# Triangular inverses of several token groups taken in one call, with other costs in the planner that orders the work, in a gated-DeltaNet and differential-attention step

## Chip, cores and metric

The kernel runs on one core of a Trainium2 chip. The metric is the time on the device in microseconds (us) for one execution of the whole program; the median of several runs counts. TensorE is called PE below, VectorE DVE, ScalarE ACT, GpSimd POOL, and SyncE, which issues most DMAs, SP.

## What is computed

One inference step through two layers, for a prompt of 2048 tokens and 8 samples of 16 tokens, model width 1024, 8 heads of width 128, all in float32. Layer 0 mixes tokens with a gated DeltaNet, layer 1 with differential attention over the prompt and a cache of 512 tokens. Around each mixer stand a modulated RMS norm, input projections, a gate and an output projection. The part the change is about is the delta rule:

```python
def gdn_chunked(q, k, v, g, beta, s0, chunk):
    G = jnp.cumsum(g, axis=-1)
    ...
    A = jnp.where(strict, jnp.einsum("bnhid,bnhjd->bnhij", kb, k) * decay, 0.0)
    eye = jnp.eye(chunk, dtype=q.dtype)
    rhs = jnp.concatenate([v * beta[..., None], kb * jnp.exp(G)[..., None]], axis=-1)
    sol = lax.linalg.triangular_solve(eye + A, rhs, left_side=True, lower=True, unit_diagonal=True)
    u_intra, w = sol[..., :dv], sol[..., dv:]
    ...
    def step(s, xs):
        u_i, w_i, qk_i, qg_i, kd_i, gl_i = xs
        u = u_i - jnp.einsum("bhcd,bhde->bhce", w_i, s)
        o = jnp.einsum("bhcd,bhde->bhce", qg_i, s) + jnp.einsum("bhij,bhje->bhie", qk_i, u)
        s = s * gl_i[..., None, None] + jnp.einsum("bhcd,bhce->bhde", kd_i, u)
        return s, o
    s_final, o = lax.scan(step, s0, xs)
```

For each head and each chunk of tokens a unit triangular matrix has to be inverted (or solved with), and then a state `s` goes through the chunks one after the other.

## The kernel before

**Tiling.** Tokens are cut into tiles of 128 (17 of them, one holds the samples). They are taken in two halves of 9 and 8 tiles. Each half of a layer is cut into groups of up to three tiles: 3, 3, 3 in the first half, and 3, 3, 2 in the second. The program goes through: start, DeltaNet heads of half 0, output projection, attention heads of half 0, output, DeltaNet heads of half 1, output projection, attention heads of half 1, output. In the trace the DeltaNet heads lie at 85 to 840 us and at 1790 to 2412 us of the span.

**The planner.** Nothing is issued in the order of the source. The class `Weave` holds the work as streams (Python generators) that yield the engine that they need next. `run` (line 281) always takes the stream that could start first (ties by priority), and `account` (line 130) charges each instruction a cost and notes when its result would be ready. The order so found is kept on each engine. Tiles and PSUM banks are taken from counted places (`tile`, `hold`, line 242 on) and are given back with `free`, so a stream can also wait for a place. Every instruction is issued through the wrapper `call` (line 105), so all rows of the profile read L105, and work is told apart by its tiles.

**A DeltaNet half** (`gdn_heads`, line 955). `projections` takes head by head and group by group; a projection is a chain of 128x384 (or 128x256) matmuls of weights `wq` or `wz` and tokens `hT`, and these are by far most of PE's work. Each group spawns `conv`, `keys`, `queries` and `values`; `keys` spawns `inverse` (line 1384) with priority 3.

**One inverse call** is for the one to three tiles of one group and one head:

- `product` makes X, the decayed product of keys, one 128x128 tile at a time.
- X goes to DRAM (area `xd`), and its 16x16 diagonal blocks, 8 for each tile, come back as `Lx`, one block to a lane, so 24 or 16 lanes are in use. `blocks` (line 1335) inverts all blocks at once with a run of 17 DVE instructions on the tiles Lx, Lw, Lt and Lr. The lanes go through DRAM (`wd`) to W16 and, masked, to W.
- PE puts the blocks together to 32, 64 and 128 rows in seven bursts of small matmuls, with ACT and DVE copies between them. In the profile they read `V,X` (32x32, all four quarters), `W,Y` (four quarters), `V,X` and `W,Y` (two quarters), transposes `cst_ident,Wf`, then `F,X` and `Wf,F`. `each` issues a burst quarter by quarter, all tiles of a quarter in a row. A float32 matmul counts twice in the profile and once in a listing of the order.
- The result is Wf, one tile of 128x128 for each token tile.

There are 48 calls: 40 of 3 tiles and 8 of 2.

**The scan** (`scans`, `scan`, line 1481 on, priority 5) then takes a head's tiles one after the other. For each tile PE makes `S,k`; DVE makes y; PE makes `y,Wf`; ACT copies r; PE makes `r,kd`; DVE makes the next state S; `S,q` and `r,E` give the output. It starts a group when that group's `inv` event is done (line 1488).

Of the kernel before, what the change touches and what calls it, by code (L numbers as in the profile page):

```python
# [87 lines left out]
class Weave:  # L88
# [23 lines left out]
    def __init__(self, tc, kept):  # L112
# [5 lines left out]
        self.parts = {}  # L118
        self.free_at = dict(pe=0.0, v=0.0, s=0.0, g=0.0, sy=0.0)
# [10 lines left out]
    def account(self, key, op, args, kw):  # L130
# [4 lines left out]
        n = 1  # L135
# [4 lines left out]
        if key == "pe":  # L140
            if op == "transpose":
                c = (2 if rest[0].dtype == F32 else 1) * max(n, out.shape[0]) * 0.417 + 2
            elif rest[0].dtype == F32:
                c = 4 * max(n, rest[0].shape[-1]) * 0.417 / (4 if out.shape[0] <= 32 else 1)
            else:
                c = max(n, 2 * rest[0].shape[-1]) * 0.417 + 2
        elif key == "v":
            fast = op in ("tensor_copy", "tensor_scalar", "memset") and all(a.space != PSUM for a in rest)
            c = 75 + n * (0.52 if fast else 1.04)
            if op in ("scalar_tensor_tensor", "tensor_scalar") and any(a.shape[-1] == 1 for a in rest):  # L150
                c += 60
            if op == "memset":
                c = 60 + 0.26 * n
        elif key == "s":
            c = 60 + 0.83 * n + (95 if "accum_out" in kw else 0)
            if any(isinstance(kw.get(k), bass.AP) for k in ("bias", "scale")):
                c += 85
            elif rest[0].space != PSUM:
                c += 32
        elif key == "g":  # L160
            if op == "memset":
                c = 30 + 0.85 * n
            elif op == "tensor_tensor":
                c = 150 + 2.1 * n
            else:
                c = (240 if len(rest) > 1 else 155) + 0.84 * n
            if op == "tensor_tensor" and kw.get("op") == ALU.pow:
                c = 300 + 160 * n
# [4 lines left out]
        start = self.free_at[key]  # L173
# [157 lines left out]
def body(ctx, tc, I, O):  # L331
# [101 lines left out]
    areas = [[dram.tile([3, n], F32, name=f"{k}{i}") for k, n in (("xd", P * P + P), ("wd", P * 16))] for i in range(2)]  # L433
# [521 lines left out]
    def gdn_heads(hi_, tiles_of, pool, ahead):  # L955
        last = hi_ == len(HALVES) - 1
        NX, NWF, NE, NV, NK, NN, ND, NU = ((3, 3, 4, 2, 5, 3, 4, 3), (3, 3, 5, 2, 6, 6, 5, 4))[hi_]
# [377 lines left out]
        def blocks(area, nl):  # L1335

            X, Wl = (pool.tile([24, 16, 16], F32, name=k, bufs=1) for k in ("Lx", "Lw"))
# [7 lines left out]
            T, R = (pool.tile([24, k], F32, name=nm, bufs=1) for k, nm in ((512, "Lt"), (64, "Lr")))  # L1345
# [38 lines left out]
        def inverse(h, gi, d):  # L1384

            nt = len(tiles_of[gi])
            h0, h1 = slice(0, 64), slice(64, P)
            X = yield from new([P, 3, P], "X", NX, "v")
            yield ("E", h, gi),
            for i in range(nt):  # L1390
# [3 lines left out]
            sy.dma_start(area[0][0:nt, 0:P * P].rearrange("t (p c) -> p t c", c=P), X[:, 0:nt])  # L1394
            yield from blocks(area, 8 * nt)
            W16 = yield from new([P, 3, 16], "W16", 2, "sy")
            sy.dma_start(W16[:, 0:nt], area[1][0:nt].rearrange("t (p c) -> p t c", c=16))
            W.free(area)
            Wt = yield from new([P, 3, 32], "W", 2, "v")
# [5 lines left out]
            V = yield from new([P, 3, 32], "V", 2, "v")  # L1405
            Y = yield from new([P, 3, 32], "Y", 2, "s")
            F = yield from new([P, 3, 64], "F", 2, "s")
# [5 lines left out]
            pa, pb, pf, pt = area_of(0, 32), area_of(96, 32), area_of(192, 64), area_of(0, 64)  # L1413
# [7 lines left out]
            def parts(t, rows, cols=slice(0, 32)):  # L1421
                cols = cols if isinstance(cols, list) else [cols] * len(rows)
                return [t[r, i, c] for r, c in zip(rows, cols) for i in range(nt)]


# [3 lines left out]
            each(parts(pa, quarters), parts(X, quarters, quarters), parts(V, quarters))  # L1429
# [10 lines left out]
            each(parts(pa, lower), parts(X, upper, lower), parts(V, upper))  # L1440
            Wf = d["Wf"] = yield from new([P, 3, P], "Wf", NWF, "g")
            e = W.either(nt * P)
            yield e
            getattr(W, e).tensor_tensor(
                out=Wf[:, 0:nt].rearrange("p t (a c) -> p t a c", c=32),
                in0=Wt[:, 0:nt, None, :].broadcast_to([P, nt, 4, 32]),
                in1=C("quart").rearrange("p (a c) -> p a c", c=32)[:, None].broadcast_to([P, nt, 4, 32]), op=ALU.mult)
# [6 lines left out]
            for r, c in zip(upper, lower):  # L1454
                s.copy(Wf[r, 0:nt, c], pb[r])

            for i in range(nt):
                yield "pe"
                pe.transpose(pf[h0, i], Wf[h0, i, h0], ident[0:64, 0:64])
# [3 lines left out]
            for c in range(64, P, 32):  # L1463
                each(parts(pt, [slice(c, c + 32)], slice(0, 64)), parts(X, [h0], slice(c, c + 32)), parts(F, [h0], h0))
            W.free(X)
            yield "s"
            s.copy(F[h1, 0:nt], pt[h1])
            yield "pe"
            each(parts(pf, [h0], h0), parts(F, [h1], h0), parts(Wf, [h1], h1))
            yield "s"  # L1470
            s.copy(Wf[h0, 0:nt, h1], pf[h0])
            W.free(Wt, V, Y, F, pi)
            W.done(("inv", h, gi))
# [188 lines left out]
    def diff_heads(hi_, tiles_of, pool, ahead):  # L1662
# [133 lines left out]

        def queries(h, gi, d):
            nt = len(tiles_of[gi])
            yield ("conv", h, gi, 0),
            yield ("sq", h, gi),  # L1800
            sq, sm = d["sq"], d["sm"]
            pt = yield from turn(d["q"], nt * P)
            yield from squares(pt, nt * P, sq[:, 1])
            W.free(pt)
            yield "g"
            g.tensor_scalar(sm[:, 3, 0:nt], sq[:, 1, 0:nt], 128.0 * EPS, 512.0 * EPS * EPS, op0=ALU.mult, op1=ALU.add)
            yield ("xq", h, gi),
            W.free(sq)
            for i in range(nt):
                yield from product(d, i, d["q"], d["E"])  # L1810
# [882 lines left out]
```

## Time and profile before

| | |
|---|---|
| median of 3 runs | 3558.8 us (3554.32 to 3575.8) |
| the profiled execution, its own time | 3559.35 us |
| its span, first to last instruction | 3557.6 us |
| mean granted clock of TensorE in it | 0.977 |
| PE busy | 3390.2 us (95%) |
| DVE, ACT, POOL busy | 2531.9 (71%), 1763.0 (50%), 1560.0 us (44%) |

Busy time on PE is time with a matmul in flight. In a view by waits, a row gives the instruction that waited, the one that released it, the time in total, how often, and the longest. In a timeline, a bracket gives the idle time of that engine before the row, and what ended it.

### The profile page before, as it was taken

The numbers are of one execution on the slowest core, as the hardware profiler recorded it, in microseconds if no ns is written. First come the engines' busy times: TensorE is split into PE (matmuls) and PEld (weight loads), VectorE is DVE, ScalarE is ACT, GpSimd is POOL, SyncE is SP. The second block draws the span as 40 slices with busy tenths as digits, with TensorE's granted clock in tenths as the row PEclk, the third lists the DMA queues.
The fourth block names the chain that finished last, engine by engine and source line by source line (L and its number), as shares of the span: only waits on it lengthen the run. The fifth ranks groups of instructions, "written<-read, shape, count | busy, mean of one in ns | idle before, by whom it ended". The sixth has DMA issues, their size and how long they took to land.

```text
span 3557.6 us, 79075 instructions
## 1 busy us (share of the span) xinstructions
PE 3390.2 (95%) x28952; PEld 3151.5 (89%) x28952; DVE 2531.9 (71%) x6462; ACT 1763.0 (50%) x5376; POOL 1560.0 (44%) x2836
## 2 busy tenths in 40 slices
PE   5999999999999999999999999998899999999988
PEld 2887789889999999998989899888898999999988
DVE  4677788776576666666567777775588878888872
ACT  3454455553354444444445555553365555555541
POOL 4344444443444344333434554544444444444432
PEclk6999999999999999999999999998999999999999
DMA  5225432236343333444432222224311112111113
GB/s 191 59 64 169 122 77 69 61 98 195 124 130 112 112 114 114 122 120 136 159 91 50 58 62 74 60 75 161 125 42 49 37 55 57 52 52 41 47 57 125
DMA packets 479420, 330.59 MB, mean 93 GB/s; under 512 B 65799, under 2 KB 442143, under 8 KB 479030
## 3 DMA queue, kind: packets, MB, share of 16 engines
q1 hardware_dynamic: 474358, 316.76, 30.0%
q0 software_dynamic: 4672, 8.78, 1.0%
q8 instruction: 227, 3.72, 0.4%
q14 instruction: 163, 1.34, 0.1%
HBM read 233.65 MB, written 91.77 MB: 91 GB/s over the span
## 4 chain that ended last, share of the span: by engine, by line
PE 37%; DVE 7%; POOL 3%; ACT 2%; issue 2%; DMA 1%; SPq 0%; POOLq 0%; DVEq 0%; ACTq 0%
PE ps L105 37%; DVE p L105 1%; DVE negm L105 1%; DVE Lt L105 1%; POOL sm L105 1%; POOL p L105 1%; POOL fo L105 1%; ACT jkg L105 0%; DVE wq L105 0%; DVE rz L105 0%; DVE Lr L105 0%; DMA st<-in_w_in_diff_dram 0%; ACT L105 0%; DMA ro<-og 0%; ACT at L105 0%
## 5 line engine op out<-in xcount | busy, mean ns | idle before, releaser
L105 PE MATMUL ps<-wq,hT 128*128 128x256 f32 x6120 | 851.4, 287 | 4.2 <-DVE r L105 3.1
L105 PEld LDWEIGHTS ps<-wq,hT 128*128 128x128 f32 x6120 | 775.2, 191 | 16.9 <-DVE r L105 3.5
L105 PE MATMUL ps<-hT,wq 128*128 128x384 f32 (+1 forms) x3456 | 696.4, 341 | 2.7 <-ACT ub L105 2.2
L105 PE MATMUL ps<-wz,hT 128*128 128x256 f32 x4488 | 647.4, 292 | 13.3 <-DVE r L105 12.1
L105 PEld LDWEIGHTS ps<-wz,hT 128*128 128x128 f32 x4488 | 581.9, 194 | 23.6 <-DVE r L105 12.8
L105 PEld LDWEIGHTS ps<-hT,wq 128*128 128x128 f32 x3456 | 557.2, 190 | 15.8 <-ACT ub L105 3.1
L105 ACT ACTIVATE p<-ps,negm 128x512 f32<-128x512 f32 (+3 forms) x640 | 397.1, 624 | 225.5 <-DVE negm L105 220.3
L105 DVE TENSOR_REDUCE negm<-ps 128x1 f32<-128x512 f32 (+3 forms) x640 | 375.0, 606 | 66.6 <-PE ps L105 55.5
L105 PE MATMUL ps<-kst,qst 128*128 128x512 f32 (+3 forms) x1280 | 346.7, 379 | 2.8 <-ACT p L105 2.7
L105 POOL TENSOR_SCALAR p<-p,fj 128x512 f32<-128x512 f32 (+2 forms) x320 | 230.8, 732 | 231.4 <-DVE fj L105 165.5
L105 PE MATMUL ps<-vpc,at 128*128 128x128 f32 x2176 | 294.9, 278 | 7.9 <-ACT at L105 6.2
L105 PEld LDWEIGHTS ps<-vpc,at 128*128 128x128 f32 x2176 | 274.5, 193 | 20.7 <-ACT at L105 10.8
L105 DVE SCALAR_TENSOR_TENSOR p<-p,fj,p 128x512 f32<-128x512 f32 (+2 forms) x320 | 248.4, 803 | 23.3 <-POOL p L105 22.8
L105 ACT COPY at<-ps 128x512 f32<-128x512 f32 (+3 forms) x258 | 132.7, 515 | 234.2 <-PE ps L105 228.9
L105 PEld LDWEIGHTS ps<-kst,qst 128*128 128x128 f32 x1280 | 205.8, 190 | 20.2 <-ACT p L105 6.0
L105 POOL TENSOR_TENSOR wq<-st,wq 128x512 fp32r<-128x512 f32 x110 | 150.5, 1370 | 162.0 <-ACT wq L105 92.0
L105 PE MATMUL ps<-cst_ident,p 128*128 128x128 f32 x1224 | 195.3, 277 | 18.9 <-DVE hT L105 7.9
L105 POOL TENSOR_TENSOR fo<-fo,cpow 128x1 f32<-128x1 f32 x280 | 175.5, 627 | 23.3
L105 ACT ACTIVATE jk<-ps 128x128 f32<-128x128 f32 (+1 forms) x212 | 80.4, 379 | 201.6 <-PE ps L105 145.6
L105 PEld LDWEIGHTS ps<-cst_ident,p 128*128 128x128 f32 x1224 | 144.7, 142 | 27.7 <-DVE hT L105 9.1
L105 POOL TENSOR_SCALAR fo<-so 128x1 f32<-128x1 f32 x144 | 32.3, 224 | 269.0 <-ACT jk L105 255.7
L105 POOL TENSOR_SCALAR fo<-so,sm 128x1 f32<-128x1 f32 x136 | 50.3, 370 | 211.5 <-ACT jkg L105 211.2
(328 smaller groups left out, 6413.2 us busy)
## 6 DMA issues: line engine op xcount, KB each, us to landing
st<-in_w_in_gdn_dram SPq DMA_DIRECT2D x128, 256.0 KB
st<-in_w_in_diff_dram SPq DMA_DIRECT2D x256, 128.0 KB
x<-x SPq DMA_DIRECT2D x34, 512.0 KB
wz<-in_w_ada_dram SPq DMA_DIRECT2D x16, 1024.0 KB
sp<-in_cache_k_dram SPq DMA_DIRECT2D x64, 256.0 KB
sp<-in_cache_v_dram SPq DMA_DIRECT2D x64, 256.0 KB
zg<-zt SPq DMA_DIRECT2D x68, 128.0 KB
og<-o SPq DMA_DIRECT2D x136, 64.0 KB
```

Of the source, the lines that this page charges most:

```text
L105: r = f(*args, **kw)
```

## The change

There are three parts.

1. **Costs in `account`.** PE: a float32r matmul of n columns costs max(n, 192) x 0.434 + 6 ns in place of max(n, twice the weights' columns) x 0.417 + 2; the other PE forms are changed alike, with less for small tiles, and a `hold` of 100 or 120 ns is put ahead of an instruction that changes the tile size of the PE array. DVE: products with a last dimension up to 8 cost twice as much. ACT: 1280 ns for a change of function table. POOL: small operations and powers cost more.
2. **Inverses in batches.** `inverse` now makes X only, and the first group of a batch spawns `invert` for all groups of the batch. Half 0: the first group alone, the second and third together; half 1: all three groups together; head 7 (the last) of either half: each group apart. So there are 27 calls (12 of 3 tiles, 7 of 6, 7 of 8, 1 of 2). Tiles, areas and lanes grow with it (up to 64 lanes), X gets 4 places in place of 3, and the tiles of a call (W16, W, F; V and Y now lie in F) have one place each in place of two. A call's three groups get their Wf together, and are free for the scan together.
3. A second, unused copy of some of the functions is taken out of the source (490 lines; no instruction depends on it).

```diff
@@ account
         if key == "pe":
+            rows, cols = (next(k for k in (32, 64, P) if a <= k) for a in (rest[0].shape[0], rest[0].shape[-1]))
             if op == "transpose":
-                c = (2 if rest[0].dtype == F32 else 1) * max(n, out.shape[0]) * 0.417 + 2
+                c = max(n, out.shape[0]) * (0.85 if rest[0].dtype == F32 else 0.65)
             elif rest[0].dtype == F32:
-                c = 4 * max(n, rest[0].shape[-1]) * 0.417 / (4 if out.shape[0] <= 32 else 1)
+                c = 4 * max(n, rest[0].shape[-1]) * 0.434 / (4 if cols == 32 else 1) / (2 if rows == 32 else 1)
             else:
-                c = max(n, 2 * rest[0].shape[-1]) * 0.417 + 2
+                c = max(n, 192) * 0.434 + 6
+
+            if (rows, cols) != self.tiling:
+                hold = 100 if self.tiling == (P, P) else 120
+                self.tiling = rows, cols
...
+            if op == "tensor_tensor" and len(out.shape) == 4 and out.shape[-1] <= 8:
+                c = 75 + 2.06 * n
...
-        start = self.free_at[key]
+        start = self.free_at[key] + hold
@@ gdn_heads
-        NX, NWF, NE, NV, NK, NN, ND, NU = ((3, 3, 4, 2, 5, 3, 4, 3), (3, 3, 5, 2, 6, 6, 5, 4))[hi_]
+        NX, NWF, NE, NV, NK, NN, ND, NU = ((4, 3, 4, 2, 5, 3, 4, 3), (4, 3, 5, 2, 6, 6, 5, 4))[hi_]
+        NTI = (6, 8)[hi_]
@@ blocks
-            X, Wl = (pool.tile([24, 16, 16], F32, name=k, bufs=1) for k in ("Lx", "Lw"))
+            X, Wl = (pool.tile([8 * NTI, 16, 16], F32, name=k, bufs=1) for k in ("Lx", "Lw"))
@@ inverse
-            X = yield from new([P, 3, P], "X", NX, "v")
+            batch = next(b for b in batches_of(h) if gi in b)
+            if gi == batch[0]:
+                W.spawn(invert(h, batch), 3)
+            X = d["X"] = yield from new([P, 3, P], "X", NX, "v")
...
+        def batches_of(h):
+
+            if h == H - 1:
+                return [[gi] for gi in range(NGr)]
+            return [[0], list(range(1, NGr))] if hi_ == 0 else [list(range(NGr))]
+
+        def invert(h, batch):
+
+            h0, h1 = slice(0, 64), slice(64, P)
+            at = [(gi, i) for gi in batch for i in range(len(tiles_of[gi]))]
+            nt = len(at)
...
+            for gi in batch:
+                yield ("X", h, gi), "sy"
+                n = len(tiles_of[gi])
+                sy.dma_start(area[0][first[gi]:first[gi] + n, 0:P * P].rearrange("t (p c) -> p t c", c=P),
+                             U[h, gi]["X"][:, 0:n])
             yield from blocks(area, 8 * nt)
...
+            F = yield from new([P, NTI, 64], "F", 1, "v")
+            V, Y = (F[:, a * NTI // 2:(a + 1) * NTI // 2].rearrange("p t (a c) -> p (t a) c", c=32) for a in range(2))
...
-            each(parts(pa, quarters), parts(X, quarters, quarters), parts(V, quarters))
+            each(parts(pa, quarters), parts_of("X", quarters, quarters), parts(V, quarters))
...
-            W.done(("inv", h, gi))
+            W.free(Wt, F, pi)
+            for gi in batch:
+                W.done(("inv", h, gi))
```

**What moves, in three places.** PE in half 1, before: the first bursts of a call of three tiles, `V,X` (12 matmuls, and later 6) and `W,Y`, among projections `wz,hT` and `hT,wq`.

```order
L105 MATMUL ps_78<-V_26499,X_25991 32x32 x12
L105 MATMUL ps_81<-wz_26269,hT_22658 128x256 x3
L105 MATMUL ps_79<-S,q_24899 128x128
L105 MATMUL ps_79<-r,E_25550 128x128
L105 MATMUL ps_75<-hT_22658,wq 128x384 x3
L105 MATMUL ps_82<-Wf_26430,F_26317 64x64 x3
L105 MATMUL ps_78<-W_26482,Y_26501 32x32 x12
L105 MATMUL ps_75<-hT_22658,wq 128x384 x9
L105 MATMUL ps_78<-V_26499,X_25991 32x32 x6
```

PE in half 1, now: the same bursts of a call of eight tiles. V and Y lie in F, so the first reads `F,X` (its 32 matmuls are listed by the X of each group, the last quarter of them here) and the second `W,F`.

```order
L105 MATMUL ps_78<-F_24281,X_23796 32x32 x3
L105 MATMUL ps_78<-F_24281,X_23827 32x32 x3
L105 MATMUL ps_78<-F_24281,X_24021 32x32 x2
L105 MATMUL ps_79<-cst_ident,v_24124 128x128 x3
L105 MATMUL ps_82<-q_24035,k_23998 128x128
L105 MATMUL ps_75<-hT_23087,wq 128x256 x3
L105 MATMUL ps_78<-W_24272,F_24281 32x32 x32
L105 MATMUL ps_75<-hT_23087,wq 128x256 x3
L105 MATMUL ps_81<-q_24035,k_23998 128x128
L105 MATMUL ps_75<-hT_23087,wq 128x256 x3
L105 MATMUL ps_80<-cst_ident,k_24160 128x128 x3
L105 MATMUL ps_75<-hT_23087,wq 128x256 x3
```

Three calls' bursts of 12 or 8 matmuls have become one of 32; all three groups' X stand in one burst. DVE at the end of half 1, before: the blocks of a call (Lt, Lr, Lw) stand between the y of a scan tile, just ahead of this piece, and its S.

```order
L105 TENSOR_TENSOR Lt<-Lx,Lw 24x64 x2
L105 TENSOR_REDUCE Lr<-Lt 24x16 x2
L105 TENSOR_TENSOR Lt<-Lw,Lr 24x64 x2
L105 TENSOR_REDUCE Lw<-Lt 24x4x4 x2
L105 TENSOR_TENSOR Lt<-Lx,Lw 24x512
L105 TENSOR_REDUCE Lr<-Lt 24x64
L105 TENSOR_TENSOR Lt<-Lw,Lr 24x512
L105 TENSOR_REDUCE Lw<-Lt 24x8x8
L105 SCALAR_TENSOR_TENSOR S<-S,g_eGl,ps_80 128x128
L105 SCALAR_TENSOR_TENSOR X_31950<-ps_79,sm_31795,E_31776 128x128
```

DVE in half 1, now: the same for a head's eight tiles, on 64 lanes, again between a y (just ahead) and its S.

```order
L105 TENSOR_TENSOR Lt<-Lx,Lw 64x64 x2
L105 TENSOR_REDUCE Lr<-Lt 64x16 x2
L105 TENSOR_TENSOR Lt<-Lw,Lr 64x64 x2
L105 TENSOR_REDUCE Lw<-Lt 64x4x4 x2
L105 TENSOR_TENSOR Lt<-Lx,Lw 64x512
L105 TENSOR_REDUCE Lr<-Lt 64x64
L105 TENSOR_TENSOR Lt<-Lw,Lr 64x512
L105 TENSOR_REDUCE Lw<-Lt 64x8x8
L105 SCALAR_TENSOR_TENSOR S<-S,g_eGl,ps_79 128x128
L105 SCALAR_TENSOR_TENSOR o_28061<-ps_82,g_eG,o_28061 128x128
```

There are as many instructions to a call as before, and 27 such runs in place of 48; 7 of them stand between a y and its own S, and 14 of the 48 did. PE at the end of half 1, before: the last projection (`wq,hT` x21), and the scans of the last head behind it.

```order
L105 MATMUL ps_77<-wq,hT_23419 128x256 x21
L105 MATMUL ps_79<-k_31157 128x128
L105 MATMUL ps_81<-S,q_30777 128x128
L105 MATMUL ps_81<-r,E_30941 128x128
L105 MATMUL ps_78<-S,k_30663 128x128
L105 MATMUL ps_82<-k_31157 128x128
L105 MATMUL ps_78<-y,Wf_31737 128x128
L105 MATMUL ps_77<-q_31219,k_31157 128x128
L105 MATMUL ps_78<-r,kd_30929 128x128
L105 MATMUL ps_80<-q_31219,k_31157 128x128
L105 MATMUL ps_79<-S,q_30777 128x128
L105 MATMUL ps_79<-r,E_30941 128x128
```

PE at the end of half 1, now: the last projection (`wq,hT` x48), and what follows.

```order
L105 MATMUL ps_79<-wq,hT_23087 128x256 x48
L105 MATMUL ps_82<-y,Wf_30427 128x128
L105 MATMUL ps_82<-r,kd_29081 128x128
L105 MATMUL ps_80<-S,q_28778 128x128
L105 MATMUL ps_80<-r,E_28954 128x128
L105 MATMUL ps_78<-S,k_28752 128x128
L105 MATMUL ps_78<-y,Wf_30427 128x128
L105 MATMUL ps_78<-r,kd_29081 128x128
L105 MATMUL ps_79<-S,q_28778 128x128
L105 MATMUL ps_79<-r,E_28954 128x128
L105 MATMUL ps_82<-S,k_28948 128x128
```

Behind the last projection stand now 13 scan tiles, `S,k` to `r,kd`, with little between them. Before, 7 stood there, with other projections (`wz,hT`) among them.

Counted over the whole program, PE's matmuls stay at 24022 (as listed). DVE goes from 6462 to 6058 instructions, ACT from 3952 to 3840, POOL from 2836 to 2764, and SP's DMAs from 1803 to 1740.

## Rows read from the trace of the kernel before

**Rows 1.** Stretches: length, busy us of PE (x), PEld, DVE, ACT, POOL, PEclk, DMA.

```profile
85.00:840.00 755.00, 731.33 (x6584) 652.38 (x6583) 571.61 (x1597) 383.01 (x1247) 329.59 (x725) 0.98 0.33 93
...
1790.00:2374.00 584.00, 565.47 (x5263) 521.72 (x5261) 450.05 (x1225) 324.26 (x1054) 288.12 (x595) 0.99 0.24 65
2374.00:2412.00 38.00, 25.98 (x228) 21.75 (x229) 25.48 (x72) 18.69 (x56) 14.77 (x29) 0.78 0.32 95
```

**Rows 2.** What PE waited for, 85 to 840 us: total, times, longest.

```profile
PE ps L105 <- DVE y L105: 5.1, 3, 2.8
...
PE ps L105 <- DVE V L105: 2.5, 5, 0.8
```

**Rows 3.** The same, 1790 to 2412 us.

```profile
PE ps L105 <- DVE S L105: 9.5, 4, 5.7
PE ps L105 <- DVE y L105: 6.1, 7, 2.8
PE ps L105 <- DVE V L105: 5.9, 2, 4.5
PE ps L105 <- ACT r L105: 3.7, 8, 0.9
```

**Rows 4.** Timeline of PE, 2245.5 to 2261 us, a call of three tiles.

```profile
2245.63 0.77 PE L105 MATMUL ps<-hT,wq 128*128 128x384 f32 x3
2246.33 0.64 PE L105 MATMUL ps<-V,X 32*32 32x32 f32 x24
2246.90 0.49 PE L105 MATMUL ps<-r,kd 128*128 128x128 f32 x2
...
2250.46 0.46 PE L105 MATMUL ps<-V,X 32*32 32x32 f32 x12
...
2255.21 0.36 PE L105 MATMUL ps<-cst_ident,Wf 64*64 64x64 f32 x3
...
2257.28 0.66 PE L105 MATMUL ps<-F,X 64*32 64x64 f32 x12
...
2259.13 0.56 PE L105 MATMUL ps<-Wf,F 64*64 64x64 f32 x6
```

**Rows 5.** Timeline of PE, 2270 to 2284 us, a call of two tiles.

```profile
2270.51 0.35 PE L105 MATMUL ps<-V,X 32*32 32x32 f32 x16
...
2274.34 0.32 PE L105 MATMUL ps<-V,X 32*32 32x32 f32 x8
...
2278.61 0.30 PE L105 MATMUL ps<-cst_ident,Wf 64*64 64x64 f32 x2
...
2281.09 0.42 PE L105 MATMUL ps<-F,X 64*32 64x64 f32 x8
...
2282.28 0.44 PE L105 MATMUL ps<-Wf,F 64*64 64x64 f32 x4
```

**Rows 6.** Costliest groups of instructions: busy us, mean ns of one, idle before.

```profile
L105 PE MATMUL ps<-hT,wq 128*128 128x384 f32 (+1 forms) x3456 | 696.4, 341 | 2.7 <-ACT ub L105 2.2
```

**Rows 7.** Timeline of DVE and PE, 2401.9 to 2412 us, two tiles' blocks.

```profile
2403.38 0.55 DVE L105 COPY Lw<-Lx 16x12 f32<-16x12 f32 x1 [4.50 <-POOL k L105]
...
2407.66 1.00 DVE L105 TENSOR_TENSOR Lt<-Lx,Lw 16x512 f32<-16x512 f32 x1
...
2411.09 0.33 DVE L105 SCALAR_TENSOR_TENSOR S<-S,g_eGl,ps 128x128 f32<-128x128 f32 x1
...
2411.47 0.80 PE L105 MATMUL ps<-S,q 128*128 128x128 f32 x2 [5.67 <-DVE S L105]
```

**Rows 8.** The same view from 2387 us: three tiles' blocks, then a scan tile.

```profile
2389.31 1.06 DVE L105 TENSOR_TENSOR Lt<-Lx,Lw 24x512 f32<-24x512 f32 x1
...
2393.28 0.46 PE L105 MATMUL ps<-S,k 128*128 128x128 f32 x2 [1.74 <-DVE S L105]
...
2395.29 0.71 PE L105 MATMUL ps<-r,kd 128*128 128x128 f32 x2 [0.39 <-ACT r L105]
...
2397.07 0.64 PE L105 MATMUL ps<-S,k 128*128 128x128 f32 x2
```

More of the change, by code (lines that the diff above doesn't have):

```diff
@@ L118, in __init__ @@
         self.parts = {}
+        self.tiling = P, P
+        self.table = None
         self.free_at = dict(pe=0.0, v=0.0, s=0.0, g=0.0, sy=0.0)
@@ L159, in account @@
                 c += 32
+            table = {AF.Silu: "silu", AF.Exp: "exp", AF.Ln: "ln", AF.Tanh: "silu exp"}.get(kw.get("func"))
+            if table and self.table not in table.split():
+                hold = 1280
+                self.table = table.split()[-1]
         elif key == "g":
@@ L432, in body @@
     vs_d = [dram.tile([P, P], F32, name=f"vsd{h}") for h in range(H)]
-    areas = [[dram.tile([3, n], F32, name=f"{k}{i}") for k, n in (("xd", P * P + P), ("wd", P * 16))] for i in range(2)]
+    areas = [[dram.tile([8, n], F32, name=f"{k}{i}") for k, n in (("xd", P * P + P), ("wd", P * 16))] for i in range(2)]
     st_d = [dram.tile([P, P], F32, name=f"std{h}") for h in range(H)]
@@ L1423, in parts, with parts_of, groups @@
                 return [t[r, i, c] for r, c in zip(rows, cols) for i in range(nt)]
+            def parts_of(name, rows, cols):
+                cols = cols if isinstance(cols, list) else [cols] * len(rows)
+                return [U[h, gi][name][r, i, c] for r, c in zip(rows, cols) for gi, i in at]
+            def groups():
+                for gi in batch:
+                    n = len(tiles_of[gi])
+                    yield U[h, gi]["Wf"], n, slice(first[gi], first[gi] + n)
             yield "v"
@@ L1439, in inverse @@
             yield "pe"
[L1440 to L1447, printed above, removed]
+            each(parts(pa, lower), parts_of("X", upper, lower), parts(V, upper))
+            for gi in batch:
+                U[h, gi]["Wf"] = yield from new([P, 3, P], "Wf", NWF, "g")
+            for Wf, n, ts in groups():
+                e = W.either(n * P)
+                yield e
+                getattr(W, e).tensor_tensor(
+                    out=Wf[:, 0:n].rearrange("p t (a c) -> p t a c", c=32),
+                    in0=Wt[:, ts, None, :].broadcast_to([P, n, 4, 32]),
+                    in1=C("quart").rearrange("p (a c) -> p a c", c=32)[:, None].broadcast_to([P, n, 4, 32]), op=ALU.mult)
             yield "s"
@@ L1453, in inverse @@
             yield "s"
[L1454 to L1459, printed above, removed]
+            for Wf, n, ts in groups():
+                for r, c in zip(upper, lower):
+                    s.copy(Wf[r, 0:n, c], pb[r, ts])
+            yield "pe"
+            for k, (gi, i) in enumerate(at):
+                pe.transpose(pf[h0, k], U[h, gi]["Wf"][h0, i, h0], ident[0:64, 0:64])
             yield "s"
@@ L1795, in rotate @@
             W.done(("k", h, t))
[L1797 to L1810, printed above, removed]
-            W.done(("qk", h, gi))
@@ L2112, in diff_heads @@
-        W.spawn(gate_columns(), 8)
-        if hi_ == 0:
-            W.spawn(cached(), 4)
-        W.spawn(loads(), 6)
-        W.spawn(other_loads(), 5.5)
-        W.spawn(scans(), 5)
-        W.spawn(projections(), 0)
-        W.spawn(others(), -1)
-        W.spawn(first_outs(0, hi_, (0, 2, 1), ((("projected",), PROJ), (("projected",), REST[2:]))), -2)
-        W.spawn(collect(0, hi_, range(NGr - 1), 384, [lambda: new([P, 384], "k", NK, "sy"), lambda: new([P, 384], "q", NK, "sy")], bank), 1)
```

456 lines of the change are left out of this document (18 added, 438 removed).

## The prediction

> **What bounds the kernel now.** I read the table of stretches first. In the DeltaNet heads PE is busy for 731.33 of 755 us in half 0 and 565.47 of 584 us in half 1; only the last 38 us of half 1 are thin, with 25.98 us busy and a granted clock of 0.78 against 0.98 and 0.99 before [rows 1]. So nearly the whole time is PE work, and there are two ways to gain here: less PE time for the same matmuls, or less of the 24 + 18.5 + 12 us in which PE stood still.
>
> Second come the waits of PE in these stretches. In half 0, the tiles of DVE among them that the change can touch are y with 5.1 us and V with 2.5 us [rows 2]. In half 1 they are S with 9.5, y with 6.1 and V with 5.9 us; ACT's r has another 3.7 us [rows 3]. V belongs to the inverses, y, S and r to the scans. DVE is not full (571.61 of 755 us [rows 1]), so its share of work is not the bound. What holds PE is that DVE does one long thing while a short one is wanted. The timeline at the end of half 1 shows it: the blocks of a call begin at 2403.38, the scan's S comes behind them at 2411.09, and PE's next matmul has waited 5.67 us for that S [rows 7].
>
> Third, the timelines of PE through one inverse call: seven bursts of small matmuls that stand one by one between projections [rows 4, 5].
>
> **Change 1: fewer bursts.** PE makes the same matmuls in 189 bursts in place of 336 (27 and 48 calls of seven), so only what a burst costs whatever its length can be saved. A call of three tiles has two bursts as 24, two as 12, and the transposes, F,X and Wf,F: 2 x 0.64 + 2 x 0.46 + 0.36 + 0.66 + 0.56 = 3.78 us [rows 4]; of two tiles 2 x 0.35 + 2 x 0.32 + 0.30 + 0.42 + 0.44 = 2.50 us [rows 5]. (W,Y I take like V,X of its size.) Around a burst something is lost too. In a run of projections each matmul lasts 341 ns but takes only 696.4 / 3456 = 202 ns of busy time, so two overlap by 140 ns [rows 6]; a burst overlaps its neighbours by 70 ns only (hT,wq ends at 2246.40, V,X starts at 2246.33; V,X ends at 2246.97, r,kd starts at 2246.90 [rows 4]). That is 2 x 70 = 140 ns a burst, say 0.13 us, or 0.9 us a call.
>
> What does one tile more cost inside a burst? From two to three tiles 3.78 - 2.50 = 1.28 us, which is 36 ns a matmul in V,X (0.29 us for 8) and 60 ns in F,X (0.24 us for 4). Taken alone this leaves nothing fixed inside the bursts (3.78 - 3 x 1.28 = -0.06). But 24 matmuls in 0.64 us are 27 ns each, so 36 is too steep for a long run; I take 30 ns, which gives 0.24 + 0.24 + 0.12 + 0.12 + 0.06 + 0.24 + 0.12 = 1.14 us a tile and a fixed part of 3.78 - 3.42 + 0.9 = 1.26 us a call. With 21 calls fewer that is 26 us; I take -25. Bounds: with 36 ns the fixed part is 0.84 us and the gain 17; if half of the loss around a burst is covered anyway, 9, say 10. At the other end the quarters of a long run go side by side and each burst pays once for a lone matmul: about 0.2 us (the transposes take 0.36 for three and 0.30 for two, so 0.18 whatever their number) and 0.13 around it, 0.33 x 7 x 21 = 48.
>
> Here a page bears on it. The rows show that 12 matmuls more in two more quarters (12 to 24) cost 0.18 us, 15 ns each, while 8 more in the same four quarters (16 to 24) cost 0.29 us, 36 ns each [rows 4, 5]. The Trainium skill, page "TensorE: Matmul & The Clock Gate", Part 3, section "The mechanism", says that a weight load overlaps matmuls in flight only when the row group differs. `each` goes quarter by quarter, so eight tiles make runs of sixteen in one row group; by that rule the steep slope of the rows goes on, and it speaks against the change: the term would be 17 us in place of 25. The trace agrees so far as it goes, with six in a row at most.
>
> **Change 2: DVE.** The blocks' run has 17 instructions whatever the lanes: the 512-wide product takes 1.00 us on 16 lanes and 1.06 on 24 [rows 7, 8]. I take 64 lanes at the same; the trace has none. A run takes up to 7.7 us (2403.38 to 2411.09 [rows 7]), so 21 fewer free DVE for over 100 us. DVE isn't the bound; what counts is the waits it causes: 5.1 + 2.5 + 9.5 + 6.1 + 5.9 = 29.1 us [rows 2, 3]. As the order shows, 7 runs stand between a y and its S in place of 14, and there are 27 in place of 48 in all. Taken in that ratio, 29.1 x 21 / 48 = 13 us go: -13. Bounds: 0 (the scans come to wait somewhere else) and -29 (all).
>
> **Change 3: the end of half 1.** All three groups of a head become ready together, so the scans lie further behind the projections. Behind the last projection stand 13 scan tiles, where there were 7. The 12 us that PE stood still there [rows 1] contain one run of blocks (5.67 us [rows 7]); the other 6.3 us are 0.9 us for each of 7 tiles. One tile alone is a chain: S,k at 2393.28, r,kd after a wait of 0.39 for r, the next S,k at 2397.07 [rows 8]. Thirteen tiles at 0.9 and one run (it still stands there for the last group) make 17.4 us: +5. Bounds: 0 if PE keeps other work, and, at 1.8 us a tile, twice as much since less stands between, 23 + 6 - 12 = +17, and with a low clock for longer (0.78 [rows 1]) +20.
>
> **Change 4: scan steps closer together.** With fewer bursts and copies in the order, more scan instructions stand right behind the one they wait for. In the two orders I count the scan steps with under about 0.7 us of PE work between: 22 before, 58 now; 39 of these are the thirteen tiles above. The other 19 against some 7 are 12 more, at 0.4 us (r 3.7 / 8 = 0.46 [rows 3]): +4 (0 to +18, if all of the 36 cost 0.5 us).
>
> **The rest.** The new costs shift the order in the attention stages as well; PE is nearly full there, and I put 0 (-8 to +8, from waits of a few us in any stage). The new SP waits (a call's DMA of X waits for three groups, with weight loads queued behind it) and the single places for W16, W and F have no price in the trace; projections for two groups lie between, so 0, and up to +8 if they don't cover.
>
> **Sum.** -25 - 13 + 5 + 4 = -29 against the profiled execution's 3559.35: 3530, or against the median 3558.8, 0.5 us lower: 3529.5. I give 3529.
>
> **Rivals.**
> *No change.* The bursts follow the steep slope (-17), and the waits on DVE only move, because a scan step is a chain whatever DVE does: -17 + 0 + 5 + 4 = -8, 3551. For it: V, S and y wait in few, long pieces (S in 4 [rows 3]), each of which another instruction can replace. Against it: half as many block runs between y and S.
> *A larger gain.* Bursts pay the fixed 0.33 us each (-48), the waits on DVE go (-29), the tail holds (0): -77, 3482. For it: 15 ns a matmul where quarters lie side by side. The same page's section "Measured speedup vs the span model" has packed matmuls starting about 4 ns apart, by which the saving would be this one; the 36 ns of the rows disagree. Against it: 36 ns a matmul in the same quarters, and a tail that the order has made longer.
> *Slower.* The scans run in blocks without projections beside them, and PE waits for one chain: bursts -10, DVE 0, short steps +18, tail +20, SP's waits +8: +36, 3595. It decides from the point where PE's standing time in half 1 goes from 30 us (18.5 + 12) to more than 60. For it: 13 lone tiles in the order, and 3.8 us for one [rows 8]. Against it: before, 7 lone tiles cost only 6 us.
>
> **How the numbers follow.** No change can be told from none within about 1%, 35.6 us: 3523 to 3594. The forecast, a gain of 15 to 50 us (3509 to 3544), has 0.50, of which 0.22 lie below 3523 and 0.28 above; the rival of no change 0.20; the larger gain 0.18; slower 0.12. Faster: 0.22 + 0.18 = 0.40; same: 0.28 + 0.20 = 0.48; slower: 0.12. The forecast's own range is 3509 to 3544; the range for 8 in 10 goes down into the larger gain (3490) and up past no change to the slower side (3568).
>
> **What would show it.** A trace of the changed kernel shows the first step right if a call of eight tiles takes about 1.3 + 8 x 1.14 = 10.4 us of PE (its first burst of 64 at 0.64 + 40 x 0.030 = 1.84 us); 2.1 us for that burst (36 ns) speaks for the steep slope, 1.2 us (15 ns) for the larger gain. The second: waits of PE for S, y and V in the two DeltaNet stretches near 16 us in sum. The third: PE standing still for about 17 us behind the last projection. The prediction is wrong if the DeltaNet stretches don't get shorter by 20 to 40 us together, or if the time comes from the attention stages.

## The result and the profile after

The changed kernel takes 3595.98 us (median of 5 runs, 3590.59 to 3608.58) against 3565.01 us for the kernel before in the same runs; the ratio is 1.0093 (1.0076 to 1.0109). It is 0.9% slower; 3529 us had been forecast. The profiled run has a span of 3591.3 us, 33.7 us more than before.

The head of the page of the kernel after (busy us and share of each engine):

```profile
span 3591.3 us, 78290 instructions
...
PE 3415.1 (95%) x28952; PEld 3192.2 (89%) x28952; DVE 2442.4 (68%) x6058; ACT 1722.1 (48%) x5240; POOL 1516.8 (42%) x2764
```

DVE, ACT and POOL have less to do, as the change meant, while PE is busy 25 us longer for the same matmuls. The stretches of the DeltaNet heads (columns as in [rows 1]; half 0, then half 1 from the last product of the attention stage ahead of it up to its own last convolution, then the rest of half 1):

```profile
85.00:814.00 729.00, 704.10 (x6260) 633.06 (x6260) 513.97 (x1419) 354.82 (x1185) 312.99 (x701) 0.95 0.31 87
...
1706.00:2382.00 676.00, 651.67 (x5941) 623.20 (x5941) 430.17 (x1036) 336.76 (x1035) 289.20 (x599) 0.98 0.28 80
2382.00:2475.00 93.00, 76.16 (x635) 64.12 (x635) 48.99 (x145) 34.22 (x125) 28.14 (x55) 0.74 0.34 98
```

Before, the granted clock in half 0 was 0.98 [rows 1]; now it is 0.95. The lengths can't be held against [rows 1]: half 1 was cut there at 1790 and 2412 us, but its last scan product (`r,E`) ends at 2444 us, and half 0 has fewer projections in its window now (x6260 for x6584 matmuls), since they have moved behind it. So I take like for like, up to the first product of the next attention stage (`kst,qst`): half 0 is 15 us longer than before and half 1 is 18 us longer. Between its first and its last product the attention stage is 12 us longer in half 0 and 9 us shorter in half 1; the end is 2 us shorter. Before, the part of half 1 behind the last convolution looked like this:

```profile
2386.00:2444.00 58.00, 46.97 (x422) 41.27 (x421) 34.74 (x94) 19.57 (x67) 21.91 (x36) 0.79 0.41 121
```

It has grown from 58 to 93 us, and its clock has fallen from 0.79 to 0.74. Over the whole program behind the first 85 us, the granted clock was at the lower of its two levels (1.2 GHz) for 107 us before and for 185 us now.

PE's waits for DVE have moved rather than gone. Half 0, against [rows 2]:

```profile
PE ps L105 <- DVE S L105: 5.9, 4, 3.5
PE ps L105 <- DVE y L105: 4.3, 9, 1.2
...
PE ps L105 <- DVE F L105: 2.4, 2, 2.1
```

Half 1, against [rows 3] (F now holds V):

```profile
PE ps L105 <- DVE y L105: 13.5, 14, 6.0
PE ps L105 <- DVE F L105: 5.9, 6, 2.2
PE ps L105 <- ACT r L105: 4.6, 9, 1.4
...
PE ps L105 <- DVE S L105: 1.4, 2, 0.7
```

S, y and V (or F) sum to 12.6 + 20.8 = 33.4 us, where the terms of before were 29.1.

**A ledger of the 33.7 us.** For each pair of successive matmuls in the two traces I took the time from end to end, and compared it with the median for the same shape in a run at full clock; small matmuls of the inverses count wholly as bursts. Idle PE (the span less the busy time): 167.4 to 176.2 us, +9. Large matmuls at the lower clock: +18. Bursts: 215.7 to 205.3, -10. What is left (a matmul right behind the one that it needs, changes of shape, instructions at the edge of a stretch): +18. The sum, 35, agrees with the spans to within rounding and edges. The two +18 are less certain than their sum: a matmul can be at the lower level for part of its time, and with another cut between the two they are +22 and +11. The -10 hides two things: at full clock the bursts cost 24 us less, and the ones at the lower clock give 14 us of that back.

### The profile page after: what moved, and what is told of

Same layout as the page of the kernel before. It is cut to its first block, busy times and chain, and to the rows that moved or that the text cites. A ratio compares the mean times of both kernels' runs of the same rounds, so it can differ in the third digit from the quotient of the medians.

```text
span 3591.3 us, 78290 instructions
## 1 busy us (share of the span) xinstructions
PE 3415.1 (95%) x28952; PEld 3192.2 (89%) x28952; DVE 2442.4 (68%) x6058; ACT 1722.1 (48%) x5240; POOL 1516.8 (42%) x2764
## 4 chain that ended last, share of the span: by engine, by line
PE 37%; DVE 7%; DMA 3%; POOL 2%; ACT 2%; issue 2%; SPq 0%; POOLq 0%; DVEq 0%; ACTq 0%
PE ps L105 37%; DVE p L105 2%; DMA E<-grow 1%; DVE negm L105 1%; POOL sm L105 0%; POOL p L105 0%; POOL fo L105 0%; DVE wq L105 0%; ACT jkg L105 0%; SPq L105 0%; DVE kst L105 0%; DMA st<-in_w_in_diff_dram 0%; DVE r L105 0%; POOL q L105 0%; DMA ro<-og 0%
## 5 line engine op out<-in xcount | busy, mean ns | idle before, releaser
L105 PE MATMUL ps<-hT,wq 128*128 128x384 f32 (+1 forms) x3456 | 682.7, 340 | 4.6 <-ACT ub L105 3.6
L105 PE MATMUL ps<-wz,hT 128*128 128x256 f32 x4488 | 639.8, 290 | 12.5 <-DVE r L105 11.7
L105 POOL TENSOR_SCALAR p<-p,fj 128x512 f32<-128x512 f32 (+2 forms) x320 | 240.2, 761 | 279.2 <-DVE fj L105 221.9
L105 POOL TENSOR_TENSOR wq<-st,wq 128x512 fp32r<-128x512 f32 x94 | 127.9, 1362 | 155.1 <-ACT wq L105 75.9
```

The source lines that it names most:

```text
L105: r = f(*args, **kw)
```

## The experiments

Medians are in us. "Ratio" is to the kernel before in the same runs, with its interval. Before was 3563 to 3565 us in all of them.

**The two parts apart.** e1 puts the old `account` into the changed kernel; e2 the new one into the kernel before; e5 only its PE part.

```diff
 e1 (27 calls), the whole of account:
-                c = max(n, 192) * 0.434 + 6
+                c = max(n, 2 * rest[0].shape[-1]) * 0.417 + 2
...
 e2 (48 calls) the whole of account, e5 (48 calls) only what stands under key == "pe":
-                c = max(n, 2 * rest[0].shape[-1]) * 0.417 + 2
+                c = max(n, 192) * 0.434 + 6
...
```

> The changed kernel with the costs of before in the planner: the 27 calls alone. Theory C (long bursts of small matmuls and the longer tail lower the granted clock, and scans bunch because a head's groups become ready together): about as slow as the changed kernel, 3580 to 3605 us, with granted half clock in the DeltaNet stretches well above the kernel before and PE's wait for y in half 1 near 13 us. Rival P (the new costs give a worse order): 3540 to 3560 us, since the bursts save some 10 us and the order is the old planner's.

> The kernel before with the new costs in the planner and its 48 calls. Theory C: 3545 to 3570 us, within 0.4% of the kernel before, half clock after 85 us within 20 us of before's. Rival P: 3580 to 3605 us.

> The kernel before with the PE part of the new costs only (float32r at 0.434 ns a column plus 6, small tiles, the 100 or 120 ns when the tile size changes); DVE, ACT and POOL costs as before, 48 calls. Theory A (the new costs of DVE, ACT and POOL spoil the order of half 0): 3545 to 3570 us. Theory B (the PE costs do it, since the planner then gives PE more time and lets others come later than they do): 3580 to 3600 us, with half 0's DeltaNet stage 25 us or more longer for the same work. Theory N (any other costs give another order, better or worse by chance): in between, with gains and losses in stages that do not match the run with all the new costs.

Measured: batches alone 3584, ratio 1.0048 (1.0035 to 1.0061); costs alone 3592, 1.0071 (1.0046 to 1.0095); PE costs alone 3619, 1.0148 (1.0127 to 1.0168). As single orders, each part costs time alone, so each of the two theories C and P seemed to name a part of the cause and neither the whole; e5 is slower than all of A, B and N had it. The truer PE costs without the others give the slowest of the three: its PE stands still for 29 us more than before's, spread over the stages. The kernels with all the new costs and no other edit of the planner (the changed kernel, e2, and e9 and e10 below) lose 11 to 14 us in the attention stage of half 0 and gain 5 to 12 us in that of half 1.

The new PE costs are the truer ones: at full clock a 128x384 matmul behind its like ends 174 ns after it in the trace of before and a 128x256 one 119 or 120 ns; the old costs say 162 and 109 ns, the new ones 173 and 117.

**How much an order is worth by luck.** The planner is greedy, so any cost moves everything behind it. I changed one constant by a nanosecond or two.

```diff
 before (e7: 3, e11: 1, e15: 4; 48 calls), e1 (e13: 3; 27 calls), e6 (e14: 3; 34 calls):
-                c = max(n, 2 * rest[0].shape[-1]) * 0.417 + 2
+                c = max(n, 2 * rest[0].shape[-1]) * 0.417 + 3
 after (e9: 5, e10: 7; 27 calls):
-                c = max(n, 192) * 0.434 + 6
+                c = max(n, 192) * 0.434 + 5
```

> The kernel before with one constant changed by nothing that matters: 3 ns in place of 2 ns added to a wide PE matmul in the planner. Theory N (the order is found greedily, so any other cost gives another order, and orders differ by luck): the time differs from before by more than 0.3%, up to 1%, with stall and half clock moved between stages. Theory B: within 0.3% of before, since the costs are the same.

> The kernel before with 1 ns in place of 2 ns added to a wide PE matmul. Theory N: 3560 to 3590 us; with the other nudge of before (3580 us) it shows how far orders of the old kind spread, and whether the kernel before sits at their fast end. If the old order was nothing special: within 0.3% of before or faster.

> The kernel before with 4 ns in place of 2. Theory N: a third order of the old kind, again slower than before, 3570 to 3605 us. If before is in the middle of its kind: as often faster, 3540 to 3565 us.

> The changed kernel with 5 ns in place of 6 ns added to a wide PE matmul in the planner. Theory N (orders differ by luck, and the order before was a lucky one of its kind): the time differs from the changed kernel's 3596 us by more than 0.3%, anywhere from 3560 to 3610 us. Theory C (the batches and the longer tail cost it whatever the order): 3585 to 3610 us, with over 70 us of half clock in the second DeltaNet stage again.

> The same with 7 ns. Theory N: another time, 3560 to 3610 us, and not the one of the other nudge. Theory C: 3585 to 3610 us, with over 70 us of half clock in the second DeltaNet stage again.

> The 27 calls with the planner's old costs, and 3 ns in place of 2 ns added to a wide PE matmul. Theory N (what a change of order does by luck is larger than what the batches do): more than 0.3% away from the 3584 us of the batches alone. Theory C (all three groups of a head in one call cost the tail of half 1 its clock): again 3575 us or more, with over 60 us of half clock in the second DeltaNet stage.

> The 34 calls (second and third group together in both halves) with the old costs, and 3 ns in place of 2. Theory C: near the 3551 us of the same without the nudge and below 3565. Theory N: more than 0.3% from it, most likely slower, 3560 to 3600 us.

| calls, costs | medians (ratios) |
|---|---|
| 48, old | before (1); 3580 (1.0047); 3604 (1.0123); 3562 (0.9997) |
| 27, old | 3584 (1.0048); 3572 (1.0020); 3580 (1.0054: e17, in the next part) |
| 34, old | 3551 (0.9958); 3549 (0.9962) |
| 48, new | 3592 (1.0071) |
| 27, new (the change) | 3596 (1.0093); 3586 (1.0063); 3597 (1.0098) |

One nanosecond makes the kernel before 1.23% slower (1.0094 to 1.0151 as ratio), no less than the whole change does. Four orders of its kind spread over 1.26%, with a mean of 1.0042: before sits at the fast end, with one of its nudges beside it. Four such orders give their mean to some 0.3% only. So what a single edit of calls or costs does is read from several orders. With the old costs, 27 calls have a mean of 1.0041, no different from 1.0042. With 27 calls, the new costs are at 1.0085 against 1.0041; the fastest of the three new ones (1.0063) lies just above the slowest of the three old ones (1.0054), which makes that likely, not certain. Theory N holds for the order of the kernel before, though one of its nudges (4 ns) changed nothing, where N had 3570 to 3605 us, and 1 ns gave more than its 3560 to 3590. The changed kernel's own orders stay within 0.35% of each other, as theory C had it and N had not; but its half clock in that DeltaNet stage was 58 and 61 us in the nudged ones, under the 70 that C expected, and 41 us in e13, whose time C missed as well.

**The call of eight and the tail.** In half 1, e6 takes the first group apart, and the second and third together, so 34 calls in all. e17 was meant to keep calls of eight but to take heads 6 and 7 group by group. Its edit changed another line, in `projections`, where the same condition says when a group's tokens (hT) count as used: in half 1 that is one head earlier now. The batches stayed as they were, 27 calls with 7 of eight tiles (64 lanes), so e17 is one more order of the 27 calls, and what it was to test stays untested. Both have the old costs.

```diff
 e6, in batches_of:
-            return [[0], list(range(1, NGr))] if hi_ == 0 else [list(range(NGr))]
+            return [[0], list(range(1, NGr))]
 e17, in projections:
-                    if h == H - 1:
+                    if h >= H - 1 - hi_:
                         used_h(gi)
```

The calls of e17, by the first copy of each run of blocks:

```profile
L105 DVE COPY Lw<-Lx x27: 155/169/436, 135.2 to 2411.4; 24x12 f32<-24x12 f32 x12, 48x12 f32<-48x12 f32 x7, 64x12 f32<-64x12 f32 x7, 16x12 f32<-16x12 f32 x1
```

> The costs of before, and in half 1 the batches of half 0: the first group apart, the second and third together (34 calls). Theory L (in half 1 a call for all eight tiles waits for three groups, so scans fall behind and the tail behind the last projection becomes a lone chain at a low clock): the tail's half clock of 51 us falls below 30 and the time is 3555 to 3572 us. Theory N: the tail's half clock stays near 50 us, the time 3575 to 3590 us.

> The batches alone (old costs), but in half 1 the last two heads group by group (29 calls). Theory L (the call of eight of head 6 makes all its scans late, so that 16 scan tiles stand behind the last projection's convolution): 8 to 11 tiles stand there, half clock in that tail falls from 31 to 51 us to under 27 us, and the time is 3545 to 3572 us. If the tail comes from the calls of eight in all heads: 16 tiles stay and the time is 3572 to 3590 us.

Measured: e6 3551, ratio 0.9958 (0.9943 to 0.9973), faster than before and than theory L's range; e17 3580, 1.0054 (1.0035 to 1.0073), which speaks for neither of its two theories. From each trace I counted the scan tiles (`y,Wf`) behind the last convolution of half 1 (the last `ub`):

| kernels | scan tiles behind it | length of that part | lower clock in it | PE idle in it |
|---|---|---|---|---|
| 48 calls (before, e7, e11, e15, e2, e5) | 7 or 8 | 41 to 59 us | 3 to 27 us | 3 to 12 us |
| 27 calls (after, e1, e9, e10, e12, e13, e17) | 16 | 89 to 98 us | 27 to 55 us | 15 to 19 us |
| 34 calls (e6, e14) | 12, 8 | 72, 49 us | 17, 13 us | 4, 2 us |

All kernels with calls of eight have both last heads' scans behind the last convolution, whatever the order; no other has more than 12. The same count at the last convolution of each head shows that the scans are late already in the heads ahead: with calls of eight 16 scan tiles, two heads, are still to come there from head 2 on (14 or 16 in head 1, counting heads from 0), with 48 calls 5 to 10, with 34 calls 8 to 13. What holds them back there (the wait for the third group, four places for X, one W, one F) wasn't taken apart. The nudged e14, same part, for comparison with the 93 us above:

```profile
2335.00:2384.00 49.00, 47.49 (x442) 44.54 (x441) 19.87 (x61) 17.75 (x62) 10.95 (x23) 0.87 0.27 79
```

How the lone chain waits is seen in the timeline of the tail of the kernel after: the y of a scan tile stands on DVE behind the blocks of the last call, an S and four `o`, two of which waited for POOL.

```profile
2437.41 0.67 DVE L105 TENSOR_REDUCE Lw<-Lt 16x64 f32<-16x512 f32 x1
...
2440.14 0.36 DVE L105 SCALAR_TENSOR_TENSOR o<-o,fo,onorm 128x128 f32<-128x128 f32 x1 [0.50 <-POOL fo L105]
2441.20 0.35 DVE L105 SCALAR_TENSOR_TENSOR o<-o,fo,onorm 128x128 f32<-128x128 f32 x1 [0.71 <-POOL fo L105]
2441.47 0.35 DVE L105 SCALAR_TENSOR_TENSOR y<-ps,g_neG,nv 128x128 f32<-128x128 f32 x1
...
2441.87 0.80 PE L105 MATMUL ps<-y,Wf 128*128 128x128 f32 x2 [6.03 <-DVE y L105]
```

**Inside a burst.** e3 (kernel before) and e12 (changed kernel) issue the same bursts tile by tile; e4 (changed kernel) cuts each burst after 12 matmuls and lets the planner put 0.6 us of other work between.

```diff
 e3, e12:
-                return [t[r, i, c] for r, c in zip(rows, cols) for i in range(nt)]
+                return [t[r, i, c] for i in range(nt) for r, c in zip(rows, cols)]
...
 e4:
+                    if k and k % 12 == 0:
+                        W.cur["at"], W.cur["by"] = W.free_at["pe"] + 600, None
+                        yield "pe"
```

> The kernel before, with each burst issued tile by tile (the quarters of a tile in a row) in place of quarter by quarter; F,X alternates its two column blocks. Same rows in the same places. If matmuls of one quarter wait for each other and those of different quarters run side by side, V,X x24 goes from 0.64 to 0.40 to 0.50 us and the kernel gains 15 to 30 us. If the order inside a burst doesn't matter, 0.64 us stays and the time is that of before within 0.3%.

> The changed kernel with every burst issued tile by tile: the same rows in the same places. If quarters of a tile run side by side in long bursts too, the burst of 64 goes from 2.0 to about 1.0 us and the kernel gains 30 to 45 us: 3550 to 3566 us. If the long bursts are what lowers the clock, the stretches at 1973, 2130 and 2283 us go as well; if the waits ahead of them do it, they stay.

> The changed kernel with each burst cut after 12 listed matmuls (24 in the profile), the next piece 0.6 us later by the planner, so that projections stand between. Theory C for the long bursts: the half-clock stretches that begin at bursts of 64 in half 1 (1973, 2130, 2283 us) and at 532 us go, and the time falls by 8 to 20 us against the changed kernel in spite of some 100 more bursts. If the long bursts are not what lowers the clock, these stretches stay and the time rises by 10 to 25 us.

Measured: e3 3534, ratio 0.9910 (0.9882 to 0.9938); e12 3537, 0.9931 (0.9909 to 0.9954), 59 us less than the changed kernel; e4 3627, 1.0165 (1.0134 to 1.0195). The bursts of a call of three tiles in e3, to hold against [rows 4]:

```profile
2220.29 0.39 PE L105 MATMUL ps<-V,X 32*32 32x32 f32 x24
...
2223.93 0.38 PE L105 MATMUL ps<-V,X 32*32 32x32 f32 x12
...
2230.57 0.53 PE L105 MATMUL ps<-F,X 64*32 64x64 f32 x12
```

V,X x24 goes from 0.64 to 0.39 us, F,X from 0.66 to 0.53, while Wf,F, which has one position only, keeps its 0.56 us. The burst of 64 in the changed kernel, where it has no wait ahead, and tile by tile in e12:

```profile
2052.81 1.91 PE L105 MATMUL ps<-F,X 32*32 32x32 f32 x64
```

```profile
2089.38 0.75 PE L105 MATMUL ps<-F,X 32*32 32x32 f32 x64 [2.28 <-DVE F L105]
```

So matmuls of one quarter follow each other at 32 ns ((1.91 - 0.64) / 40), and those of changing quarters at 9 ns on average ((0.75 - 0.39) / 40). The Trainium skill, page "TensorE: Matmul & The Clock Gate", Part 3, "The mechanism", has weight loads overlap matmuls in flight only where the row group differs; these rows agree, with the two paces beside it. The section "Measured speedup vs the span model" of the same page of the Trainium skill has about 4 ns between packed matmuls; the 9 ns here are float32 in two passes, and the trace decides.

The clock shows in the same places. At 2128 us of the changed kernel PE has waited 2.22 us for F, and the long burst follows; at 2206 us the same kind of call comes without a wait; in e12 at 2089 us the wait is there, 2.28 us, and the burst is short. The timeline and the stretches (1.2 GHz is a clock of 0.5):

```profile
2128.77 2.34 PE L105 MATMUL ps<-F,X 32*32 32x32 f32 x64 [2.22 <-DVE F L105]
...
2133.36 3.06 PE L105 MATMUL ps<-W,F 32*32 32x32 f32 x64
...
2207.00 1.91 PE L105 MATMUL ps<-F,X 32*32 32x32 f32 x64
```

```profile
2128.00:2141.00 13.00, 12.23 (x180) 11.24 (x180) 7.30 (x18) 5.00 (x19) 2.37 (x5) 0.61 0.17 47
2206.00:2219.00 13.00, 13.00 (x213) 12.11 (x212) 11.40 (x27) 6.31 (x22) 6.39 (x12) 1.00 0.40 107
```

```profile
2089.00:2102.00 13.00, 12.41 (x250) 11.56 (x251) 11.73 (x28) 8.05 (x27) 6.77 (x14) 1.00 0.31 83
```

In these three calls neither a wait of 2.2 us alone nor a burst of 1.9 us alone lowered the clock; both together did. The other traces bear this out. The six kernels with calls of eight and bursts quarter by quarter (the changed kernel, e1, e9, e10, e13, e17) have 42 such first bursts: 21 came without a wait (under 0.1 us), and the clock fell within 4 us behind the start of none of them; 7 came behind a wait of 0.98 to 2.22 us, and it fell so in 6; of the 14 in between it fell in 5. In e12 it fell in none of 7, with waits of up to 2.28 us. Cutting the bursts (e4) didn't help: the order is another, the DeltaNet stage of half 1 has 113 us at the lower clock, and the bursts cost 20 us more, probably since each cut pays its way in and out. So theory C's remedy failed, and more bursts cost more; what lowers the clock in e4 was not settled.

**What beats both.** e8 has old costs up to the DeltaNet heads of half 1 and new ones from there on, batches in half 0 only, and bursts tile by tile. e16 is e6 (34 calls) with bursts tile by tile and the new costs in the last attention stage only; e18 is e16 with the nudge to 3 ns.

```diff
+                (w.account if w.new else w.account_before)(key, op, args, kw)
 e8, in gdn_heads:    + W.new = W.new or hi_ == 1
 e16, e18, in diff_heads:   + W.new = hi_ == 1
```

> Costs of before up to the DeltaNet heads of half 1, the new costs from there on; batches in half 0 only (second and third group together), half 1 group by group; every burst tile by tile. If the parts add as the stages of the runs so far say (bursts by tile -30, new costs in half 1 and behind it -20, batches in half 0 -3): 3505 to 3525 us, faster than both kernels. If the gains in half 1 were luck of one order: 3525 to 3550 us.

> The 34 calls with the old costs up to the attention stage of half 1 and the new costs in that stage only, every burst tile by tile. The order of the DeltaNet stages is that of the 34 calls at 3551 us. If bursts by tile bring 35 to 45 us on it and the new costs 5 to 10 us in the last attention stage: 3500 to 3515 us, faster than both kernels and than the mixed one at 3517. If the faster bursts only move waits: 3515 to 3535 us.

> The fastest kernel so far with 3 ns in place of 2 ns in the old costs' wide PE matmul. If its time rests on calls of six and on bursts by tile, and not on one order: 3480 to 3510 us, over 1.5% faster than before again. If it was a lucky order: 3510 to 3535 us.

Measured: e8 3517, ratio 0.9864 (0.9842 to 0.9886); e16 3494, 0.9804 (0.9778 to 0.9829); e18 3499, 0.9826 (0.9800 to 0.9852). e16 is 2% faster than before and 2.9% (0.9804 / 1.0093) faster than the changed kernel, and its nudged order holds, so it isn't one lucky order. Against e6 it gains 3551 - 3494 = 57 us. Of these, 8 us lie in the last attention stage with its new costs (888 to 880 us from its first to its last product in the two traces); the other 49 us, with the bursts tile by tile, lie between the 30 us of e3 and the 59 us of e12.

## Why the prediction was wrong

**Right: the price of bursts (change 1).** The forecast for a call of eight was 10.4 us; at full clock its seven bursts cost 2.03 + 2.03 + 1.22 + 1.22 + 0.76 + 1.90 + 1.27 = 10.43 us in the trace, measured as before by the ends of the matmuls around them. A call of six takes 8.1. That makes the gain 24 us at full clock, where 25 were forecast. The pace taken, 30 ns, was right (32); the steep 36 ns, from two to three tiles, didn't go on. What the step missed is that a long burst behind a wait can come at the lower clock: some 565 of the inverses' matmuls did, where 205 had before, and 14 of the 24 us were lost.

**Wrong: the waits on DVE (change 2, -13).** The waits on S, y and V or F went from 29.1 to 33.4 us, +4. Scaling them by the number of block runs took the waits for a property of those runs; they hang on what stands ahead of a scan's y and S on DVE, and in the longest of them, 6.03 us in the tail, that was another run and four `o`. The rival "no change" had named just that, waits that only move. (The 64 lanes were as free as assumed: below.)

**Half right: the tail (change 3, +5).** The tail did grow, in idle time almost as forecast: 93 - 76.16 = 16.8 us against 17.4 forecast, and 58 - 46.97 = 11.0 us before. It holds 16 scan tiles by the convolution, 13 by the projection, so that the two sizes come so close is partly luck. The step counted idle time only; the clock (0.74, 48 us at the lower level where it was 24) was kept for the upper bound, and it is about as large again: 24 us more at half speed are 12 us at most.

**Not measured alone: the short steps (change 4, +4), SP's waits and the single places (0).** PE's waits for r in half 1 went from 3.7 [rows 3] to 4.6 us. What matmuls right behind the ones that they need cost without a wait can't be told from the rest of the last +18 of the ledger. No run took the other two apart.

**The step that failed most: "the rest", 0 with -8 to +8.** Against the sum of -29 the ledger has +35. Of the 64 us between them the bursts are 15 (-10 in place of -25), and idle PE is 13 (+9 in place of -13 + 5 + 4 = -4). The other 36 us, the two +18, stand for large matmuls at the lower clock, short steps and changes of shape all over the program, which the sum put at nothing: it had a clock only in the upper bound of the tail, and a new order only in the attention stages. There it was right on balance (+12 and -9). The 15 and 18 us more lie in the two DeltaNet parts with the projections behind them, which the forecast wanted 20 to 40 us shorter together.

Behind that 0 stood the unspoken assumption that the order of the kernel before is an ordinary one and that a new order, with truer costs, is as good. Nudges of 1 to 2 ns move the kernel before by 0 to +1.2%; it lies 0.42%, 15 us, under the mean of its four orders. And truer PE durations didn't make a better order: PE costs alone, in the one order tried, are the slowest of all kernels with uncut bursts, 1.0148. By the means of the table, an estimate, the +0.93% of the change is 0.42% for the luck given up, nothing for the 27 calls, whose saved bursts the tail and the clock take back, and some 0.4% for the costs. Each of these is no larger than what one order can scatter, so the split is likely and not shown.

That the forecast's rival "slower" came true, with 3595 us for 3596 measured, is luck. It was to decide from 60 us of standing PE in half 1; that is 41 us now (24.3 + 16.8). Its mechanism, scans without projections beside them, is there in the tail, with 6 us more of idle PE and up to 12 us of clock, but SP's +8 is not: PE's waits for the weights `wz` in half 0 fell from 4.6 to 2.3 us.

## What to carry to other kernels

Where a greedy planner sets the order, nudge one cost by a nothing and time the result a few times before believing any edit under one or two per cent; a tuned order can be a lucky one, and a change then pays for losing it. Batching small matmuls to save their fixed cost pays only as far as the batch doesn't make the consumers later: in half 1 calls of three and five tiles gained where calls of eight did not. Order the matmuls inside a burst so that neighbours use different parts of the array; here a few lines of Python were worth 30 us in the kernel before and 59 us in the changed one.

## What was new about the hardware

32x32 matmuls of one quarter in a row come at 32 ns, of changing quarters at 9 ns on average, so a burst of 64 takes 1.91 or 0.75 us. A burst of that size takes 3.06 us at the lower clock, and the granted clock fell to that level behind 6 of 7 waits of 0.98 to 2.22 us followed by a burst of 1.9 us, though behind none of 21 such bursts without a wait, nor behind waits of up to 2.28 us followed by a burst of 0.75 us. It also fell without a wait to speak of: at 532 us PE had been busy for the whole of 525 to 533 us, with small matmuls, transposes of nine columns and a few wide ones, and then ran 34 of the next 38 us at the lower level:

```profile
525.00:533.00 8.00, 8.00 (x140) 5.75 (x138) 4.47 (x14) 1.23 (x3) 0.00 (x0) 0.97 0.59 181
533.00:546.00 13.00, 12.19 (x116) 8.73 (x116) 6.01 (x16) 5.43 (x18) 4.33 (x4) 0.63 0.72 228
```

On 64 lanes the DVE products took as long as on 24 (1.06 us [rows 8]), as had been assumed:

```profile
1882.79 1.05 DVE L105 TENSOR_TENSOR Lt<-Lx,Lw 64x512 f32<-64x512 f32 x1
```
